# The second mixer's output projection in two column pairs: one more seven-product unit, and other homes for its sums, its recombined input and its spare weight buffer

## The chip, the cores and the metric

The kernel runs on one core of a Trainium2 chip, in one launch. The metric is the device time of that core in microseconds (us). The core's engines run side by side and wait for each other through semaphores: PE (TensorE, the matrix products), DVE (VectorE), ACT (ScalarE), POOL (GpSimd), and SP, which here only issues DMA transfers. On-chip memory is SBUF; products add up in PSUM banks.

## The reference

An encoder of two layers over 256 positions and a model width of 2048, all in float32: layer 0 has grouped-query attention, layer 1 a mixture of dilated window attentions, and each is followed by a gated MLP. The change lies in the last line of the second layer's mixer:

```python
wts = jax.nn.softmax(jnp.stack(log_zs, axis=0), axis=0)
y = jnp.concatenate([wts[g][..., None] * outs[g] for g in range(n_g)], axis=2)
y = y.reshape(b, s, B_WIDTH).astype(h.dtype)
return y @ w_o
```

`y` has 256 rows and 3072 columns (three groups of eight heads of 128), `w_o` is 3072 by 2048. The result is added to the residual `h`, and the MLP of that layer follows, with a root-mean-square norm before it.

## The kernel before

**Split products.** Every float32 factor is split into a rounded high part and a low remainder, and a product is three matrix products: high by high, high by low, low by high. The input's parts lie ready. A weight tile of 128 x 1024 (512 KB) is loaded into a buffer `raw` by SP, then ACT rounds it into `wh` (line 147 or 182) and DVE makes `wl = raw - wh` (line 148 or 183). There are four `wh` and four `wl` buffers (`NHL`), so a split can begin when PE is done with the tile four places before it.

**Plain chunks.** The projection's depth of 3072 is six chunks of 512 (`kg` 0 to 5), its width four column blocks of 512 (`n`). One chunk of one block is a call of `feed`: two loads, two splits, and 24 matmuls (four depth steps, two halves of the 256 rows, three products), so 12 matmuls a weight tile. Chunk `2*g+hf` is made by attention group `g` in half `hf` of the heads, so chunks 0, 2, 4 are there early, and 1, 3, 5 come from the last value stage, which runs beside the start of this projection.

**Seven-product units.** `fast_unit` takes one chunk for two column blocks at once, as a two-by-two matrix product of blocks (rows halves by column blocks) done with seven products in place of eight (Winograd's form of Strassen's scheme): 42 matmuls in place of 48. It loads the same four weight tiles, but makes four sums of them on DVE (line 181: into three `sum` tiles named by `spot`, and one in place), and splits seven tiles in place of four; each split tile serves six matmuls. It needs the chunk's input in a recombined form, `recombined(kg, ...)`: two additions (line 927), four subtractions of half their size (line 934) and one split (lines 323 and 324), kept in `own` tiles. `pair` runs a column pair: it keeps four accumulators (two row halves for each block) and, from the first unit on, four more PSUM banks for products 1, 5, 6 and 7. After the pair's last unit `closing` folds these four into the result (lines 202 to 214: one copy on ACT, four sums on DVE from PSUM, four additions to `h`), beside the accumulators' own additions to `h` (line 464).

**The stage before the change.** Blocks 0 and 1 go through `project2`: chunks 0, 2, 4 for block 0, then for block 1; then all that is left of the value stage is issued and the recombinations of chunks 0 and 2 are started; then chunks 1, 3, 5 for block 0 and for block 1. All of it is plain. Then `pair` runs blocks 2 and 3: chunks 1 and 3 plain for both, chunk 0 as a unit, chunk 4 plain for both, chunk 2 as a unit, chunk 5 plain for both. When a block is added to `h`, ACT takes its sums of squares (line 370) and `late_transpose` turns it into the next stage's input: DVE transposes (line 380), copies of 32 x 256 by POOL (line 399) and ACT (line 401), and a split per 128 columns (lines 334 and 337).

**Weight buffers.** `raw_tile` hands out four `raw` buffers in turn; while `extra[0]` names a pool and tags, every third tile is put into one of those instead. In blocks 0 and 1 there are only the four; in blocks 2 and 3 the tags are `e0` and `e1` (both free once the value stage's `v12` tiles are read), so six buffers, each used again six tiles later. The scheduler sets the order on every engine, SP's queue included, from the order in which the code runs and a head start (`AHEAD`) for the splits. SP's queue is served in its order, and a load waits there until its buffer's last reader is done.

Of the kernel before, what the change touches and what calls it, by code (L numbers as in the profile page):

```python
# [36 lines left out]
def tile_encoder(ctx: ExitStack, tc: tile.TileContext, x, xT, w_a, w_ao, q_gain, k_gain, w_b, w_bo,  # L37
# [25 lines left out]
    def nm(s):  # L63
        uid[0] += 1
        return f"{s}_{uid[0]}"
# [15 lines left out]
    def start(gen):  # L81
        if next(gen, StopIteration) is not StopIteration:
            pending.append(gen)
# [242 lines left out]
    def split(hi, lo, src):  # L326
        if lo is None:
            copy(hi, src)
            return
        nc.scalar.activation(hi, src, AF.Copy)  # L330
        nc.vector.tensor_tensor(lo, src, hi.bitcast(F32), ALU.subtract)  # L331
# [16 lines left out]
    def pair_tile(pool, shape, tag, bufs=1, whole=False):  # L348
        if whole:
            return pool.tile(shape, F32, tag=tag + "h", name=nm(tag), bufs=bufs), None  # L350
        return tuple(pool.tile(shape, F32R, tag=tag + c, name=nm(tag + c), bufs=bufs) for c in "hl")
# [542 lines left out]
    def out_proj(w, slots, kgs, late, g_next, junk, pool, tag, new_quad, cuts=(), units=None):  # L894
        hTn, ss = {}, new_ss()

        def post(n):
            sumsq_cols(ss, n, junk)
            start(late_transpose(hTn, n, g_next, pool, tag, new_quad))

        def done(accs, n):
            add_residual(accs, n)
            post(n)

        if units:
            fast, own, tmp, spot, folds, raws = units
            done(project2(w, 0, 1, slots, kgs, late, lambda a: done(a, 0), None, cuts,
                          [lambda kg=kg: recombined(kg, slots, own, tmp) for kg in fast]), 1)
            extra[0] = raws
            both = {kg: [(kg, 0), (kg, 1)] for kg in sorted(kgs) if kg not in fast}  # L910
            (k0, k1, k2, k3), (f0, f1) = both, fast
            pair(w, (2, 3), slots, both[k0] + both[k1] + [(f0, None)] + both[k2] + [(f1, None)] + both[k3],
                 spot, folds, post)
            extra[0] = None
            drain(1)
            return hTn, ss
        done(project2(w, 0, 1, slots, kgs, late, lambda a: done(a, 0), None, cuts), 1)
        for n in (2, 3):
            done(project(w, n, slots, kgs), n)
        return hTn, ss  # L920
# [330 lines left out]
    def mixer_b(hT, ss_in):  # L1251
        with tc.tile_pool(name="bpool", bufs=1) as bp:
# [34 lines left out]
            def fold_tile():  # L1287
                return bp.tile([P, 2, 512], F32, tag="vh", name=nm("fold"))

            cw, turn = load_taps(1)  # L1290
            allp = slice(None)
            for hf in range(2):
# [77 lines left out]
                def value_stage(hf=hf, probs=probs, e=e, vs=vs):  # L1370
# [40 lines left out]
                    def times_v(g, heads):  # L1411
                        for i in heads:
                            if i % 2 == 0:
                                outs[g] = ps_tile()
                            o = outs[g][:, i % 2 * NT:(i % 2 + 1) * NT]
                            pT = pTs.pop(i) if g == 0 else turned.pop((g, i))
                            for kt in range(2):
                                sel = (allp, kt, slice(i * P, (i + 1) * P))
                                if g == 0:
                                    mm3(o, vs[g], pT, sel, (allp, slice(kt * NT, (kt + 1) * NT)), kt == 0, kt == 1)  # L1420
                                else:
                                    nc.tensor.matmul(o[:, kt * P:(kt + 1) * P], vs[g][0][sel],  # L1422
                                                     pT[:, kt * P:(kt + 1) * P], start=True, stop=True)
                        for i in heads:
                            sl = (2 * g + hf) * 4 + i
                            if i % 2 == 0:
                                slots.update(new_slots((sl, sl + 1)))
                            split(*slots[sl], outs[g][:, i % 2 * NT:(i % 2 + 1) * NT])

                    yield  # L1430
                    for n in range(2):
# [21 lines left out]
                    for g in (1, 2):  # L1453
                        for i in range(0, 4, 2):
                            times_v(g, (i, i + 1))
                            yield
                        if g == 1:
                            yield

                for g in range(3):  # L1460
                    bts = biases(hf, g)
# [27 lines left out]
                    if g == 0:  # L1489
                        start(value_stage())  # L1490

            def own(kg):
                return pair_tile(bp, [P, 4, NT], "qT" if kg else "kT")

            def spot(i):
                t = ("vh", 1) if i == 0 else ("pT", 2)
                return bp.tile([P, 2, 512], F32, tag=t[0], name=nm("sum"), bufs=t[1])

            def folds():
                return [bp.tile([P, 2, 512], F32, tag=t, name=nm("fold")) for t in ("btg", "vh")]  # L1500

            return *out_proj(w_bo, slots, [0, 2, 4, 1, 3, 5], 3, 3, junk, bp, "vl", lambda: quad_tile(bp, "stg", 2),
                             (), ((0, 2), own, tmp, spot, folds, (bp, ["e0", "e1"]))), cw

    hT, ss, cw = mixer_a()
    hT, ss = ffn(0, hT, ss, cw, 2, False, bias_lines)
# [86 lines left out]
```

## Time and profile before

| what | value |
|---|---|
| time, median of 3 runs | 2223.64 us (2222.51 to 2224.64) |
| profiled execution: its time | 2222.29 us |
| profiled execution: its span | 2220.5 us |
| PE busy, share of the span | 2207.1 us, 99% |
| DVE busy | 1823.1 us, 82% |
| ACT busy | 1528.2 us, 69% |
| loads of `w_bo` | 48, of 512 KB |

The span runs from the first to the last instruction; the execution's time holds 1.8 us more around it. PE's busy share counts pipelined matmuls, whose records overlap: the distance from one start to the next is what one more costs. The projection of the change lies between 1374.9 us (its first product) and about 1510 us. A row of the timeline reads: start, duration, engine, line, operation, tiles written and read, count, and in brackets the idle time before it and what ended it.

### The profile page before, as it was taken

What the parts mean: (1) busy time and instruction counts of PE and PEld (TensorE: products, weight loads), DVE (VectorE), ACT (ScalarE), POOL (GpSimd) and SP (SyncE); (2) the same over time, 40 slices, a digit from 0 to 9 for tenths busy, and PEclk for the clock granted to TensorE, in tenths of its full rate; (3) what the DMA queues carried; (4) which work ended last, traced back from release to release, by engine and by line L of the source; (5) the groups of instructions that cost most, each with busy time, mean ns of one, the idle gap of its engine ahead of it and who ended that gap; (6) DMA issues with size and microseconds to landing.
All of it is one profiled execution on the core that took longest, in us unless ns stands there. A gap on an engine that the chain in (4) does not pass through costs nothing.

```text
span 2220.5 us, 28992 instructions
## 1 busy us (share of the span) xinstructions
PE 2207.1 (99%) x9933; PEld 1828.5 (82%) x9933; DVE 1823.1 (82%) x2295; ACT 1528.2 (69%) x2328; POOL 546.1 (25%) x793
## 2 busy tenths in 40 slices
PE   9999999999999999999999999999999999999998
PEld 7888888888888888888888888888888888888887
DVE  6877669899897998868876878587798998879887
ACT  7666677787457787677756775567777855678764
POOL 3343222321003221042354216003222300212211
PEclk9999999999999999999999999999999999999999
DMA  8665665656656566665666555556555565656754
GB/s 305 192 220 184 216 188 190 201 189 196 203 181 222 186 205 200 204 202 195 183 199 199 174 180 189 190 184 214 181 202 194 192 209 190 217 162 218 224 193 143
DMA packets 126181, 439.60 MB, mean 198 GB/s; under 512 B 14408, under 2 KB 18248, under 8 KB 126032
## 3 DMA queue, kind: packets, MB, share of 16 engines
q1 hardware_dynamic: 123056, 429.05, 59.2%
q0 software_dynamic: 2688, 8.39, 1.5%
q8 instruction: 78, 1.28, 0.2%
q14 instruction: 71, 0.58, 0.1%
q10 hardware_dynamic: 288, 0.30, 0.0%
HBM read 432.34 MB, written 5.34 MB: 197 GB/s over the span
## 4 chain that ended last, share of the span: by engine, by line
PE 54%; POOL 1%; issue 1%; DMA 0%; ACT 0%; DVE 0%; POOLq 0%; DVEq 0%; ACTq 0%
PE acc L136 15%; PE acc L135 15%; PE acc L137 15%; PE ps L190 1%; PE ps L189 1%; PE ps L191 1%; PE acc L190 1%; PE acc L189 1%; PE acc L191 1%; DMA raw<-in_w_b_dram 0%; POOL wide L399 0%; PE ps L1422 0%; PE ps L342 0%; POOL wide L384 0%; ACT wh L147 0%
## 5 line engine op out<-in xcount | busy, mean ns | idle before, releaser
L148 DVE TENSOR_TENSOR wl<-raw,wh 128x1024 fp32r<-128x1024 f32 (+1 forms) x700 | 858.9, 1237 | 257.6 <-ACT wh L147 253.1
L147 ACT ACTIVATE wh<-raw 128x1024 fp32r<-128x1024 f32 (+1 forms) x700 | 726.8, 1046 | 342.5 <-PE acc L137 240.6
L136 PE MATMUL acc<-wl,xh 128*128 128x512 f32 x1984 | 773.8, 390 | 1.5 <-DVE wl L148 1.4
L135 PE MATMUL acc<-wh,xh 128*128 128x512 f32 x1984 | 773.7, 390 | 0.5 <-ACT wh L147 0.5
L137 PE MATMUL acc<-wh,xh 128*128 128x512 f32 x1984 | 772.1, 389 | 0.0
L136 PEld LDWEIGHTS acc<-wl,xh 128*128 128x128 f32 x1984 | 372.6, 188 | 81.5 <-DVE wl L148 5.7
L135 PEld LDWEIGHTS acc<-wh,xh 128*128 128x128 f32 x1984 | 372.5, 188 | 77.4 <-ACT wh L147 1.0
L137 PEld LDWEIGHTS acc<-wh,xh 128*128 128x128 f32 x1984 | 372.4, 188 | 76.9
L632 POOL COPY u<-quad 32x256 f32<-32x256 f32 x352 | 237.7, 675 | 702.5 <-DVE quad L380 684.4
L135 PE MATMUL acc<-wh,a 128*128 128x512 f32 x720 | 280.9, 390 | 0.0
L136 PE MATMUL acc<-wl,a 128*128 128x512 f32 x720 | 280.3, 389 | 0.0
L137 PE MATMUL acc<-wh,a 128*128 128x512 f32 x720 | 280.0, 389 | 0.0
L182 ACT ACTIVATE wh<-raw 128x1024 fp32r<-128x1024 f32 x140 | 148.5, 1061 | 122.4 <-PE acc L137 102.6
L183 DVE TENSOR_TENSOR wl<-raw,wh 128x1024 fp32r<-128x1024 f32 x140 | 166.9, 1218 | 6.3 <-ACT wh L182 5.8
L632 ACT ACTIVATE u<-quad 32x256 f32<-32x256 f32 x352 | 147.8, 420 | 23.2 <-DVE quad L380 18.7
L137 PEld LDWEIGHTS acc<-wh,a 128*128 128x128 f32 x720 | 135.1, 188 | 28.3 <-DVE a L331 0.2
L135 PEld LDWEIGHTS acc<-wh,a 128*128 128x128 f32 x720 | 135.2, 188 | 27.7
L136 PEld LDWEIGHTS acc<-wl,a 128*128 128x128 f32 x720 | 135.2, 188 | 27.6 <-DVE wl L148 0.3
L399 POOL COPY wide<-quad 32x256 f32<-32x256 f32 x88 | 54.8, 622 | 234.8 <-DVE quad L380 167.8
L492 ACT ACTIVATE stg<-acc,rstd 128x512 f32<-128x512 f32 x122 | 81.9, 685 | 32.9 <-PE acc L137 21.3
L384 POOL COPY wide<-quad 32x256 f32<-32x256 f32 x133 | 89.8, 675 | 41.4 <-DVE quad L380 32.0
L380 DVE STREAM_TRANSPOSE quad<-stg 128x512 f32<-128x512 f32 x112 | 75.7, 696 | 11.6 <-ACT stg L492 11.4
(318 smaller groups left out, 2444.5 us busy)
## 6 DMA issues: line engine op xcount, KB each, us to landing
raw<-in_w_up_dram SPq DMA_DIRECT2D x352, 512.0 KB, 4.6
raw<-in_w_down_dram SPq DMA_DIRECT2D x176, 512.0 KB, 4.6
raw<-in_w_b_dram SPq DMA_DIRECT2D x144, 512.0 KB, 4.6
raw<-in_w_bo_dram SPq DMA_DIRECT2D x48, 512.0 KB, 4.4
raw<-in_w_a_dram SPq DMA_DIRECT2D x40, 512.0 KB, 4.7
raw<-in_w_ao_dram SPq DMA_DIRECT2D x32, 512.0 KB, 4.5
raw<-in_w_a_dram SPq DMA_DIRECT2D x16, 256.0 KB, 5.8
there<-quad POOLq DMA_DIRECT2D x6, 512.0 KB, 3.7
```

Source lines behind the costliest of these rows:

```text
L135: nc.tensor.matmul(accs[m], xh, wh[:, j, :], start=st, stop=False)
L136: nc.tensor.matmul(accs[m], xh, wl[:, j, :], start=False, stop=False)
L137: nc.tensor.matmul(accs[m], xl, wh[:, j, :], start=False, stop=sp)
L147: nc.scalar.activation(wh[:, c], r[:, c], AF.Copy)
L148: newest[0] = nc.vector.tensor_tensor(wl[:, c], r[:, c], wh[:, c].bitcast(F32), ALU.subtract)
L182: nc.scalar.activation(wh, r, AF.Copy)
L183: newest[0] = nc.vector.tensor_tensor(wl, r, wh.bitcast(F32), ALU.subtract)
L380: nc.vector.transpose(quad[:, :, at, :], src.rearrange("p (x c t) -> p c x t", c=4, t=32))
L384: nc.gpsimd.tensor_copy(o[32 * c:32 * c + 32, :, 32 * q:32 * q + 32], quad[32 * q:32 * q + 32, c])
L399: nc.gpsimd.tensor_copy(dst, src)
L492: evac[0] = nc.scalar.activation(o[:, m, :], accs[m], AF.Copy, scale=rstd[:, m:m + 1])
L632: put(u[32 * c:32 * c + 32, :, :, 32 * q:32 * q + 32], quad[32 * q:32 * q + 32, c].rearrange("p (j m) t -> p j m t", m=2))
```

## The change

Blocks 0 and 1 become a `pair` too, with chunk 2 as a seven-product unit in it; the second pair keeps its two units (chunks 0 and 2). The recombination of chunk 2 (`made(2)`) is put beside the value stage as soon as that has made the last heads of group 0 (chunk 1); that of chunk 0 is started between the two pairs. Chunks are marked in `ready` when they are made, and `pair` issues pending work until the chunk that it wants is marked. The homes change: the recombined inputs move from `kT`/`qT` to `qT` (chunk 0) and `v` (chunk 2); the first weight sum from `vh` to `kTh`; the second fold tile from `vh` to `kTl`; the wide tile of the transposed blocks from `vl` to `e1`. The spare weight buffer is then `e0` alone, named twice, so that it has one place: every third weight tile, from the end of the value stage on, goes into this one place. In `mixer_b`:

```diff
+            ready = {0, 4}
+
+            def made(kg):
+                def own(kg):
+                    return [bp.tile([P, 4, NT], F32R, tag=("v", "qT")[kg == 0] + c, name=nm("own")) for c in "hl"]
+
+                yield from recombined(kg, slots, own, tmp)
+                ready.add(kg)
+
+            def spot(i):
+                t = ("kTh", 1) if i == 0 else ("pT", 2)
+                return bp.tile([P, 2, 512], F32, tag=t[0], name=nm("sum"), bufs=t[1])
+
+            def folds():
+                return [bp.tile([P, 2, 512], F32, tag=t, name=nm("fold")) for t in ("btg", "kTl")]
...
+                        if heads[-1] == 3 and hf == 1:
+                            ready.add(2 * g + hf)
+                            if g == 0:
+                                beside.append(made(2))
...
+                    if hf == 1:
+                        ready.add("u")
+                        extra[0] = bp, ["e0", "e0"]
...
-            def own(kg):
-                return pair_tile(bp, [P, 4, NT], "qT" if kg else "kT")
-
-            def spot(i):
-                t = ("vh", 1) if i == 0 else ("pT", 2)
-                return bp.tile([P, 2, 512], F32, tag=t[0], name=nm("sum"), bufs=t[1])
-
-            def folds():
-                return [bp.tile([P, 2, 512], F32, tag=t, name=nm("fold")) for t in ("btg", "vh")]
-
-            return *out_proj(w_bo, slots, [0, 2, 4, 1, 3, 5], 3, 3, junk, bp, "vl", lambda: quad_tile(bp, "stg", 2),
-                             (), ((0, 2), own, tmp, spot, folds, (bp, ["e0", "e1"]))), cw
+            return *out_proj(w_bo, slots, [0, 2, 4, 1, 3, 5], 3, 3, junk, bp, "e1", lambda: quad_tile(bp, "stg", 2),
+                             (), (made, spot, folds, ready)), cw
```

In `out_proj`:

```diff
         if units:
-            fast, own, tmp, spot, folds, raws = units
-            done(project2(w, 0, 1, slots, kgs, late, lambda a: done(a, 0), None, cuts,
-                          [lambda kg=kg: recombined(kg, slots, own, tmp) for kg in fast]), 1)
-            extra[0] = raws
-            both = {kg: [(kg, 0), (kg, 1)] for kg in sorted(kgs) if kg not in fast}
-            (k0, k1, k2, k3), (f0, f1) = both, fast
-            pair(w, (2, 3), slots, both[k0] + both[k1] + [(f0, None)] + both[k2] + [(f1, None)] + both[k3],
-                 spot, folds, post)
+            made, spot, folds, ready = units
+            both = {kg: [(kg, 0), (kg, 1)] for kg in kgs}
+            pair(w, (0, 1), slots, both[0] + both[4] + both[1] + both[3] + [(2, None)] + both[5], spot, folds, post,
+                 0, ready)
+            ready.discard(0)
+            start(made(0))
+            pair(w, (2, 3), slots, both[1] + both[3] + [(0, None)] + both[4] + [(2, None)] + both[5],
+                 spot, folds, post, 0, ready)
             extra[0] = None
             drain(1)
             return hTn, ss
```

What stands where now, at the places that the prediction speaks of. In these rows a weight tile's name ends in the number of its allocation; `wl` is a split, `sum` and a `raw` written from `raw` are the unit's sums.

First, DVE at the first column pair's fifth chunk. Before, in a plain stretch of block 1:

```order
L148 TENSOR_TENSOR wl_2435_12926<-raw_2429_12902,wh_2434_12925 128x1024
L934 TENSOR_TENSOR tmp_2415_12821<-tmp_2414_12820,tmp_2415_12821 128x256 x2
L148 TENSOR_TENSOR wl_2441_12953<-raw_2438_12948,wh_2440_12952 128x1024
L148 TENSOR_TENSOR wl_2443_12971<-raw_2439_12950,wh_2442_12970 128x1024
L148 TENSOR_TENSOR wl_2447_12993<-raw_2444_12988,wh_2446_12992 128x1024
```

Now, from the third plain tile before the unit to the unit's fourth split:

```order
L148 TENSOR_TENSOR wl_2421_12851<-raw_2417_12832,wh_2420_12850 128x1024
L148 TENSOR_TENSOR wl_2425_12871<-raw_2422_12866,wh_2424_12870 128x1024
L181 TENSOR_TENSOR sum_2436_12914<-raw_2432_12906,raw_2435_12912 128x1024
L148 TENSOR_TENSOR wl_2427_12887<-raw_2423_12868,wh_2426_12886 128x1024
L183 TENSOR_TENSOR wl_2440_12918<-raw_2432_12906,wh_2439_12917 128x1024
L181 TENSOR_TENSOR raw_2435_12912<-raw_2435_12912,raw_2434_12910 128x1024
L183 TENSOR_TENSOR wl_2442_12928<-raw_2433_12908,wh_2441_12927 128x1024
L181 TENSOR_TENSOR sum_2437_12915<-sum_2436_12914,raw_2434_12910 128x1024
L183 TENSOR_TENSOR wl_2444_12938<-raw_2434_12910,wh_2443_12937 128x1024
L181 TENSOR_TENSOR sum_2438_12916<-sum_2437_12915,raw_2433_12908 128x1024
L183 TENSOR_TENSOR wl_2446_12949<-sum_2436_12914,wh_2445_12948 128x1024
```

A stretch with splits and little else now holds the unit's sums between its splits. `raw_2423_12868` and `raw_2434_12910` share the one place `e0`: the second is loaded when the split that reads the first (`wl_2427_12887`) is done.

Second, DVE at the last unit of the second pair (chunk 2). Before, from the last two plain tiles on:

```order
L148 TENSOR_TENSOR wl_2534_13412<-raw_2531_13407,wh_2533_13411 128x1024
L148 TENSOR_TENSOR wl_2536_13428<-raw_2532_13409,wh_2535_13427 128x1024
L181 TENSOR_TENSOR sum_2541_13451<-raw_2537_13443,raw_2540_13449 128x1024
L183 TENSOR_TENSOR wl_2545_13455<-raw_2537_13443,wh_2544_13454 128x1024
L181 TENSOR_TENSOR raw_2540_13449<-raw_2540_13449,raw_2539_13447 128x1024
L183 TENSOR_TENSOR wl_2547_13465<-raw_2538_13445,wh_2546_13464 128x1024
L181 TENSOR_TENSOR sum_2542_13452<-sum_2541_13451,raw_2539_13447 128x1024
```

Now, from the plain stretch's first split on:

```order
L148 TENSOR_TENSOR wl_2539_13392<-raw_2536_13387,wh_2538_13391 128x1024
L148 TENSOR_TENSOR wl_2541_13408<-raw_2537_13389,wh_2540_13407 128x1024
L148 TENSOR_TENSOR wl_2549_13440<-raw_2546_13435,wh_2548_13439 128x1024
L337 SCALAR_TENSOR_TENSOR xh_2542_13423<-wide_2529_13338,gain_76,xh_2542_13423 128x256
L337 SCALAR_TENSOR_TENSOR xh_2543_13426<-wide_2529_13338,gain_76,xh_2543_13426 128x256
L337 SCALAR_TENSOR_TENSOR xh_2544_13429<-wide_2529_13338,gain_76,xh_2544_13429 128x256
L337 SCALAR_TENSOR_TENSOR xh_2545_13432<-wide_2529_13338,gain_76,xh_2545_13432 128x256
L148 TENSOR_TENSOR wl_2551_13456<-raw_2547_13437,wh_2550_13455 128x1024
L181 TENSOR_TENSOR sum_2556_13479<-raw_2552_13471,raw_2555_13477 128x1024
L183 TENSOR_TENSOR wl_2560_13483<-raw_2552_13471,wh_2559_13482 128x1024
L183 TENSOR_TENSOR wl_2562_13493<-raw_2553_13473,wh_2561_13492 128x1024
L181 TENSOR_TENSOR raw_2555_13477<-raw_2555_13477,raw_2554_13475 128x1024
```

The four splits of a transposed block now stand between the units, and `raw_2536_13387`, `raw_2547_13437` and `raw_2554_13475` share `e0`.

Third, SP's queue at the same place, before:

```order
L125 DMA raw_2525_13371<-in_w_bo_dram 128x1024
L125 DMA raw_2526_13373<-in_w_bo_dram 128x1024
L125 DMA raw_2531_13407<-in_w_bo_dram 128x1024
L125 DMA raw_2532_13409<-in_w_bo_dram 128x1024
L170 DMA raw_2537_13443<-in_w_bo_dram 128x1024
```

and now:

```order
L125 DMA raw_2537_13389<-in_w_bo_dram 128x1024
L125 DMA raw_2546_13435<-in_w_bo_dram 128x1024
L125 DMA raw_2536_13387<-in_w_bo_dram 128x1024
L170 DMA raw_2552_13471<-in_w_bo_dram 128x1024
L170 DMA raw_2553_13473<-in_w_bo_dram 128x1024
L125 DMA raw_2547_13437<-in_w_bo_dram 128x1024
L170 DMA raw_2555_13477<-in_w_bo_dram 128x1024
```

The loads stood in the order of use; now the loads into `e0` (13387, 13437) stand two or three places later than their use, behind loads into the four other buffers.

## The prediction

> **What bounds the kernel now.** I read the page's busy shares first, then what PE waited for in the stage, then busy time by stretch, and last the timelines of DVE, ACT and SP's loads around the second pair, where two units of the new kind already run.
>
> ```profile
> span 2220.5 us, 28992 instructions
> PE 2207.1 (99%) x9933; PEld 1828.5 (82%) x9933; DVE 1823.1 (82%) x2295; ACT 1528.2 (69%) x2328; POOL 546.1 (25%) x793
> ```
>
> ```profile
> PE acc L136 <- DVE wl L148: 0.3, 1, 0.3
> ```
>
> ```profile
> core 0: us, PE busy (x) PEld busy (x) DVE busy (x) ACT busy (x) POOL busy (x), PEclk, DMA share, GB/s
> 1410.00:1457.00 47.00, 47.00 (x210) 38.89 (x209) 32.41 (x39) 32.25 (x51) 8.97 (x16) 1.00 0.58 189
> 1457.00:1499.00 42.00, 42.00 (x187) 34.79 (x186) 37.78 (x34) 24.30 (x24) 0.00 (x0) 1.00 0.56 180
> ```
>
> PE bounds: it is idle for 2220.5 - 2207.1 = 13.4 us of the whole span, and between 1340 and 1560 us, around the projection, it waits once, for 0.3 us. So there is next to nothing to win but the products themselves. The two stretches show what a unit costs the others: in plain chunks (1410 to 1457) DVE has 47.0 - 32.4 = 14.6 us free, with two units in 42 us (1457 to 1499) 4.2 us.
>
> ```profile
> 1465.61 0.39 PE L189 MATMUL ps<-wh,a 128*128 128x512 f32 x1
> ...
> 1467.64 0.39 PE L189 MATMUL acc<-wh,a 128*128 128x512 f32 x1
> ```
>
> Between these starts lie nine matmuls: (1467.64 - 1465.61) / 9 = 0.226 us each, though each record is 0.39 us long. A plain weight tile (12 matmuls) keeps PE 2.71 us, a tile of a unit (6) 1.36 us.
>
> ```profile
> 1457.25 1.23 DVE L181 TENSOR_TENSOR sum<-raw,raw 128x1024 f32<-128x1024 f32 x1 [0.88 <-DMA raw<-in_w_bo_dram]
> 1458.39 1.22 DVE L148 TENSOR_TENSOR wl<-raw,wh 128x1024 fp32r<-128x1024 f32 x1
> 1459.53 1.22 DVE L181 TENSOR_TENSOR raw<-raw,raw 128x1024 f32<-128x1024 f32 x1
> 1460.66 1.22 DVE L181 TENSOR_TENSOR sum<-sum,raw 128x1024 f32<-128x1024 f32 x1
> 1461.80 1.22 DVE L183 TENSOR_TENSOR wl<-raw,wh 128x1024 fp32r<-128x1024 f32 x1
> ...
> 1479.94 1.23 DVE L181 TENSOR_TENSOR sum<-raw,raw 128x1024 f32<-128x1024 f32 x1 [2.29 <-DMA raw<-in_w_bo_dram]
> ```
>
> ```profile
> 1457.64 1.06 ACT L182 ACTIVATE wh<-raw 128x1024 fp32r<-128x1024 f32 x1 [1.58 <-PE acc L137]
> ```
>
> ```profile
> DMA to landing us min/median/max: 3.6/4.4/5.5
> ```
>
> A DVE sum or split takes 1.22 us, but the next starts after 1.14 (1458.39, 1459.53, 1460.66). ACT's rounding takes 1.06 and waits for PE to leave the buffer four tiles back. A load of 512 KB lands 3.6 to 5.5 us after its issue, 4.4 in the median of the 48. Both units already make DVE wait for a load, 0.88 and 2.29 us, with six buffers; PE does not feel it.
>
> **The change part by part.** *Products.* One chunk of blocks 0 and 1 takes 42 matmuls in place of 48: 6 x 0.226 = 1.36 us less on PE, the engine that sets the end. (The mean busy time of 0.39 would make it 2.3; the spacing is what counts.) The second pair keeps its units, so this is all.
>
> *DVE and ACT.* The new unit has 7 splits for 4, and 4 sums: 7 more operations, 7 x 1.14 = 8.0 us on DVE; on ACT three more roundings, 3 x 1.06 = 3.2 us. Closing the pair adds the eight operations of lines 204 to 214.
>
> ```profile
> 1502.48 0.68 DVE L210 TENSOR_TENSOR h<-h,fold 128x512 f32<-128x512 f32 x1
> 1503.08 0.68 DVE L211 TENSOR_TENSOR h<-h,fold 128x512 f32<-128x512 f32 x1
> 1503.68 1.30 DVE L380 STREAM_TRANSPOSE quad<-h 128x512 f32<-128x512 f32 x2
> ```
>
> At 0.60 from start to start they are 4.8 us. Together 12.8 us, against the 14.6 that DVE had free in the plain stretch: covered on average, with little over. On ACT the 3.2 us and one copy lie in 47.0 - 32.3 = 14.7 us of idle time. If that cover were gone, every 1.14 us of DVE would be 1.14 us on PE.
>
> *Order.* Chunk 1 is wanted after eight tiles in place of twelve, 8 x 2.71 = 21.7 us after the first product at 1374.91, so at 1396.6; chunk 3 at 1407, chunk 5 later still.
>
> ```profile
> 1376.05 0.38 DVE L331 TENSOR_TENSOR a<-ps,a 128x256 fp32r<-128x256 f32 x1
> ...
> 1394.61 0.42 DVE L331 TENSOR_TENSOR a<-ps,a 128x256 fp32r<-128x256 f32 x1 [0.45 <-ACT a L330]
> ```
>
> The first row ends chunk 1, the second chunk 5, the last of all. Nothing is late: I cost this at nothing. The recombinations are the same two; that of chunk 2 moves into DVE's idle time before 1400, that of chunk 0 stands between the pairs. Loads are the same 48, and the homes taken over (`kTh`, `kTl`, `vl`'s successor `e1`) belong to the value stage that is over by then: nothing.
>
> *The spare buffer* is the term that can cost. With `e0` alone, every third tile has one place, so its load waits for the split three tiles earlier, then come landing, ACT's 1.06 and DVE's split: 4.4 + 1.06 + 1.22 = 6.7 us a round, against 3 x 2.71 = 8.1 us of plain PE work, but only 4.1 us in a unit. Before, each place had six tiles' time. And DVE works in order: a sum that waits for such a load holds up all splits behind it. I follow the three units by hand in the order of rows shown above, with 4.4 us of landing.
>
> *Unit of the first pair.* Let PE leave the seventh plain tile before the unit at time 0. ACT and DVE finish the third-last tile (`wl_2421`) at 1.06 + 1.22 = 2.3; that frees the place for the unit's `raw_2435`, which lands at 6.7; its sum ends at 7.8, the last plain split (`wl_2427`) at 9.0; only now is `e0` free for `raw_2434`: 13.4. The sum into `raw_2435` waits for it; with the operations behind it up to the fourth split (`wl_2446`) that is 6 x 1.14: 20.2. PE has six plain tiles and three of the unit until then, 16.3 + 4.1, and needs the low part one matmul later: 20.6. Margin 0.4 us; and the landing stands in it twice.
>
> *First unit of the second pair.* The start is the same, to 9.0 us; its four sums then stand early and the load into `e0` is in time. Its fourth split comes after five more operations, two, four and one small ones between, at about 19.2: margin 1.4. But POOL's sixteen copies of two transposed blocks fall here.
>
> ```profile
> 1447.86 1.40 DVE L148 TENSOR_TENSOR wl<-raw,wh 128x1024 fp32r<-128x1024 f32 x1 [0.67 <-ACT wh L147]
> ```
>
> Beside such copies a split took 1.40, not 1.22. For nine operations that is 1.6 us: a loss of about 0.2 us, from 0 to 0.5. The Trainium skill ("SBUF — State Buffer", Who interferes with whom) says more: a VectorE operation with two SBUF inputs and a GpSimd operation that reads SBUF share a port pair, and the second to issue "fully blocks" until the first is done. The row above shows 0.18 us of it; what full blocking would give is a rival below.
>
> *Second unit of the second pair.* Let DVE finish the unit before at time 0, with PE just waiting for it. The first plain split ends at 1.14 and frees `e0`; `raw_2547` lands at 5.5, is rounded at 6.6 and split at 7.8 (the other two splits and the four of line 337 fit in between). `raw_2554` lands at 12.2; the sum that waits for it and four more operations end the fourth split at 12.2 + 5.7 = 17.9. PE needs it after 1.36 + 4 x 2.71 + 3 x 1.36 + 0.2 = 16.5. So PE waits 1.4 us, less what lead the unit before left it (some 0.4). Again two landings are in it.
>
> *Sum.* At 4.4 us: 0 + 0.2 + 1.0 = 1.2 us of new waits. With loads as fast as 3.6: none. With 5.5: 1.8 + 1 + 3.6 = 6.4. In a unit loads come in fours, and run into each other:
>
> ```profile
> DMA to landing us min/median/max: 3.7/4.9/5.5
> ```
>
> These are the loads issued between 1460 and 1480, in the second pair. Some of the loads into `e0` will have company, some not; I take 4.6: 0.1 + 0.3 + 1.6 = 2.0 us. So -1.36 + 2.0 = +0.6 us: the span becomes 2221.1. The profiled execution took 2222.29, which is 1.35 under the median of the three; from the median, 2223.64 + 0.6 = 2224.2 us. The bounds: 2223.64 - 1.4 = 2222.3 and 2223.64 - 1.4 + 6.4 = 2228.6.
>
> *Between the pairs* PE's first matmul into block 2 waits for block 0's additions to `h` (line 464), which stand on DVE behind five splits and the fold's four sums; the fifth split reads `e0` again. Counted from the unit's last split: two splits to 2.3, load and rounding to 7.8, split 8.9, addition 9.5; PE gets there after the unit's last tile and four plain ones, 1.4 + 10.8 = 12.2. Margin 2.7 us: nothing.
>
> **The rivals.** *The products are simply saved.* If the loads into `e0` land in under 4.1 us, or DVE gains lead elsewhere, no unit waits: 2222.3 us. For it: PE felt nothing of the waits of 0.88 and 2.29 us. Against: those had six places. The Trainium skill ("DMA: Bandwidth & Descriptors", Anatomy of one DMA) fits 2.0 us + bytes/436e3, an estimate of 3.2 us for 512 KB on GpSimd's path; the fastest here took 3.6, so by the trace it is not that quick.
>
> *The single place decides (slower).* If the landings of the loads that share `e0` average 5.2 us or more, the first and the last unit each lose two times the excess: at 5.3, 1.4 + 0.9 + 3.2 = 5.5; and in plain chunks the round of 5.3 + 2.3 = 7.6 us leaves only 0.5 of 8.1 to catch up, so that a lag of the first pair is carried into the second, 1 us more: -1.4 + 6.5 = +5.1, 2228.7 us. For it: the maximum of 5.5, and 4.9 as the median of twenty microseconds. Against: a place that is served late makes fewer loads run side by side.
>
> *POOL's copies block DVE.* Were every one of the nine operations held for half a copy (the eight at 1447.35 took 4.35 us, 0.54 each, so 0.3), that is 2.4 us more in the second pair's first unit and, its lead gone, 0.4 in the next: 2224.2 + 2.4 = 2226.6.
>
> ```profile
> 1447.35 4.35 POOL L399 COPY wide<-quad 32x256 f32<-32x256 f32 x8 [10.02 <-DVE quad L380]
> ```
>
> *It gains more than the products,* because the reordering also takes away waits: these are 0.3 us in the whole stage, so a gain of over 0.2% is not to be had this way.
>
> **How the numbers follow.** The forecast has 0.48, the plain saving 0.24, the single place 0.18, the blocking copies 0.08, a larger gain 0.02. About 0.2% (4.4 us) is what a measurement of this kernel can tell from no change. Faster by more: 0.02. Slower by more, over 2228.1: the single place, and a little of the others: 0.19. Within: 0.79. The range goes from the plain saving with half a microsecond of the runs' own spread, 2221.8, to 2228.8, a little past the single place's price, and leaves out about 0.1 at each end.
>
> **What would show it.** Right: PE with six matmuls fewer; in the first pair's unit and in the second pair's last one, PE waiting for DVE's `wl` of line 183 for some tenths to 1.5 us, and ahead of it DVE idle for a load of `w_bo` at line 181, 3 us and more, the load issued only when the split three tiles before was done. Wrong: PE waits at line 135 or 1438 (readiness, the order), at lines 202 to 214 or 464 (the accumulators come free late), or DVE never idle for loads while PE waits. The forecast itself is wrong if PE's new waits in the stage are under 0.7 or over 5.8 us.

## The result, and the profile after

| kernel | time, median | range | runs |
|---|---|---|---|
| before | 2223.64 us | 2221.76 to 2225.1 | 11 |
| changed | 2230.2 us | 2225.22 to 2232.12 | 11 |

The ratio is 1.0028, 95% interval 1.0020 to 1.0035: the changed kernel is slower by 0.28%, 6.6 us between the medians. Predicted were 2224.2 us and a range to 2228.8. The profiled execution took 2229.77 us.

The page of the changed kernel, span and busy line:

```profile
span 2228.0 us, 29016 instructions
PE 2209.2 (99%) x9927; PEld 1827.7 (82%) x9927; DVE 1834.0 (82%) x2310; ACT 1530.5 (69%) x2332; POOL 548.1 (25%) x793
```

The six matmuls are gone (9933 to 9927). What PE waited for between 1340 and 1560 us (engine, tile and line, what ended the wait; us in total, times, longest), where it had waited once for 0.3 us:

```profile
PE ps L190 <- DVE wl L183: 2.8, 4, 0.9
PE acc L190 <- DVE wl L183: 1.3, 3, 0.6
PE acc L136 <- DVE wl L148: 1.0, 1, 1.0
```

Line 190 is a unit's matmul with the low part: in a unit PE waits seven times for DVE's split. Line 136 is here a product of the MLP behind the projection, with a late split, some 9 us after the MLP's first product (1513.30 us); that place is called "the joint" below. Busy time by stretch tells where; the columns are the stretch and its length, then busy time of PE, weight loads, DVE, ACT and POOL, and the granted clock. First before, then after:

```profile
1440.00:1460.00 20.00, 20.00 (x90) 16.57 (x89) 15.48 (x21) 14.57 (x25) 4.06 (x8) 1.00 0.58 185
1460.00:1480.00 20.00, 20.00 (x90) 16.57 (x89) 16.29 (x15) 11.69 (x11) 0.00 (x0) 1.00 0.65 206
```

```profile
1400.00:1440.00 40.00, 40.00 (x178) 33.06 (x177) 28.16 (x27) 18.17 (x19) 0.00 (x0) 1.00 0.57 184
1440.00:1460.00 20.00, 20.00 (x90) 16.57 (x89) 18.68 (x25) 13.77 (x23) 4.65 (x5) 1.00 0.64 192
1460.00:1480.00 20.00, 16.93 (x69) 11.95 (x68) 16.41 (x17) 13.60 (x22) 11.11 (x11) 1.00 0.45 150
1480.00:1500.00 20.00, 18.95 (x82) 14.85 (x81) 17.82 (x19) 13.71 (x19) 1.07 (x2) 1.00 0.58 186
1500.00:1525.00 25.00, 24.03 (x107) 19.56 (x105) 23.82 (x34) 19.07 (x35) 9.71 (x15) 1.00 0.48 155
```

The clock is the same. PE loses most between 1460 and 1480, in the first unit of the second pair, and less in the second unit and at the joint. DVE is no busier there than before (16.41 and 16.29), so it is not short of time: it waits too. POOL, which had nothing to do there, now works for 11.11 us. The timelines of POOL, ACT and DVE in the changed kernel show what they wait for:

```profile
1455.18 9.02 POOL L399 COPY wide<-quad 32x256 f32<-32x256 f32 x8 [72.86 <-PE acc L137]
1472.72 8.39 POOL L399 COPY wide<-quad 32x256 f32<-32x256 f32 x8 [8.52 <-DVE quad L380]
```

```profile
1458.87 2.13 ACT L401 ACTIVATE wide<-quad 32x256 f32<-32x256 f32 x5
1464.23 0.51 ACT L334 ACTIVATE xh<-wide,gain 128x256 fp32r<-128x256 f32 x1 [3.24 <-POOL wide L399]
1464.65 1.04 ACT L182 ACTIVATE wh<-raw 128x1024 fp32r<-128x1024 f32 x1
...
1472.65 0.84 ACT L401 ACTIVATE wide<-quad 32x256 f32<-32x256 f32 x2 [2.92 <-DVE quad L380]
1473.52 1.06 ACT L182 ACTIVATE wh<-raw 128x1024 fp32r<-128x1024 f32 x1
```

```profile
1462.52 1.42 DVE L181 TENSOR_TENSOR sum<-sum,raw 128x1024 f32<-128x1024 f32 x1
1465.72 1.23 DVE L183 TENSOR_TENSOR wl<-raw,wh 128x1024 fp32r<-128x1024 f32 x1 [1.79 <-ACT wh L182]
...
1474.61 1.26 DVE L183 TENSOR_TENSOR wl<-raw,wh 128x1024 fp32r<-128x1024 f32 x1 [0.94 <-ACT wh L182]
```

Read from the bottom: DVE's first split of the unit waits 1.79 us for ACT's rounding (line 182). That rounding stands in ACT's queue behind the scaled split of block 0's transposition (line 334), which waits 3.24 us for POOL's eight copies; and these took 9.02 us. Later ACT is stopped again, 2.92 us, by block 1's first copy, which waits for DVE's transposition (line 380), and that stands on DVE between the unit's splits. Before, POOL's eight copies had taken 5.20 us for block 0 and 4.35 for block 1 (1447.35 to 1451.70), and all were over when the unit began at 1465.61. Block 0's, before:

```profile
1432.13 5.20 POOL L399 COPY wide<-quad 32x256 f32<-32x256 f32 x8 [49.66 <-DVE quad L380]
```

**A finer yardstick.** Single runs of one kernel differ by up to 7 us, more than what is to be told apart. The table under the experiments therefore also has the length of the stage in each trace: from the start of one matmul ahead of the projection (1372.15 us before) to the start of the same matmul in the MLP behind it (1600.18 us), 228.03 us before. Changed: 1373.66 to 1607.81, 234.15 us, so +6.12. The products alone would make it 1.36 shorter; 6.12 + 1.36 = 7.48 us is lost to waits. The rest of the 7.5 us between the two profiled spans lay already ahead of the stage (1373.66 against 1372.15). By a gap I mean what lies between two matmul starts beyond the 0.227 us of their spacing: in the changed kernel 3.9 us in the first unit of the second pair, 1.4 in its second unit, 1.1 at the joint (0.45 before); what is left of the 7.5 are delays of under a quarter of a microsecond each.

### The profile page after: what moved, and what is told of

It is laid out like the page before. It is cut to its first block, busy times and chain, and to the rows that moved or that the text cites. A ratio compares the mean times of both kernels' runs of the same rounds, so it can differ in the third digit from the quotient of the medians.

```text
span 2228.0 us, 29016 instructions
## 1 busy us (share of the span) xinstructions
PE 2209.2 (99%) x9927; PEld 1827.7 (82%) x9927; DVE 1834.0 (82%) x2310; ACT 1530.5 (69%) x2332; POOL 548.1 (25%) x793
## 4 chain that ended last, share of the span: by engine, by line
PE 51%; DVE 2%; POOL 1%; issue 1%; DMA 1%; ACT 1%; POOLq 0%; DVEq 0%; ACTq 0%
PE acc L136 14%; PE acc L135 14%; PE acc L137 14%; PE ps L190 1%; PE ps L191 1%; PE ps L189 1%; PE acc L190 1%; PE acc L191 1%; PE acc L189 1%; POOL wide L399 1%; DMA raw<-in_w_b_dram 0%; DVE wl L148 0%; PE ps L1438 0%; PE ps L342 0%; DVE wl L183 0%
## 5 line engine op out<-in xcount | busy, mean ns | idle before, releaser
L135 PE MATMUL acc<-wh,a 128*128 128x512 f32 x704 | 274.7, 390 | 0.0
L136 PE MATMUL acc<-wl,a 128*128 128x512 f32 x704 | 274.2, 390 | 0.0
L137 PE MATMUL acc<-wh,a 128*128 128x512 f32 x704 | 273.8, 389 | 0.0
L183 DVE TENSOR_TENSOR wl<-raw,wh 128x1024 fp32r<-128x1024 f32 x144 | 171.9, 1218 | 8.5 <-ACT wh L182 8.1
L137 PEld LDWEIGHTS acc<-wh,a 128*128 128x128 f32 x704 | 132.1, 188 | 27.5 <-DVE a L331 0.2
L135 PEld LDWEIGHTS acc<-wh,a 128*128 128x128 f32 x704 | 132.2, 188 | 27.1
```

What stands on the lines that cost most here:

```text
L135: nc.tensor.matmul(accs[m], xh, wh[:, j, :], start=st, stop=False)
L136: nc.tensor.matmul(accs[m], xh, wl[:, j, :], start=False, stop=False)
L137: nc.tensor.matmul(accs[m], xl, wh[:, j, :], start=False, stop=sp)
L183: newest[0] = nc.vector.tensor_tensor(wl, r, wh.bitcast(F32), ALU.subtract)
```

## The experiments

Theory A is the one place of the spare weight buffer, on which the prediction rested. Theory B is the reading above: ACT's in-order queue, blocked by the transposition of blocks 0 and 1. Later came B2 (it matters how late the blocks are finished), C (the new unit's own work) and D (DVE has no time left). "Lost" is the stage's difference plus 1.36 us where the unit saves its products. Each median is of 5 to 11 runs; each ratio is to the runs of the kernel before in the same series, whose medians were 2223.64 to 2224.36 us; each stage is that of one trace.

| kernel | median, us | ratio to before (95%) | stage | lost |
|---|---|---|---|---|
| before, one spare place | 2223.84 | 1.0002 (0.9993 to 1.0011) | -0.01 | 0.0 |
| changed | 2230.2 | 1.0028 (1.0020 to 1.0035) | +6.12 | 7.5 |
| changed, two spare places | 2228.08 | 1.0020 (1.0011 to 1.0028) | +3.86 | 5.2 |
| changed, transposition behind the unit | 2229.69 | 1.0032 (1.0020 to 1.0043) | +4.89 | 6.3 |
| the same, two spare places | 2229.93 | 1.0027 (1.0016 to 1.0037) | +5.85 | 7.2 |
| changed, no copies on POOL | 2232.03 | 1.0034 (1.0022 to 1.0046) | +6.77 | 8.1 |
| changed, first pair plain | 2227.69 | 1.0017 (1.0009 to 1.0026) | +2.98 | 3.0 |
| changed, early recombination | 2232.36 | 1.0034 (1.0021 to 1.0046) | +7.04 | 8.4 |
| changed, blocks two chunks apart | 2226.79 | 1.0013 (1.0004 to 1.0022) | +1.68 | 3.0 |
| changed, blocks four chunks apart | 2223.88 | 0.9999 (0.9990 to 1.0007) | -0.71 | 0.7 |
| the same kernel again | 2223.68 | 0.9997 (0.9988 to 1.0006) | -0.70 | 0.7 |
| four chunks apart, two spare places | 2223.67 | 1.0000 (0.9991 to 1.0009) | -0.86 | 0.5 |
| four chunks apart, early recombination | 2223.6 | 0.9995 (0.9986 to 1.0004) | -0.82 | 0.5 |

**One spare place in the kernel before.**

```diff
-                             (), ((0, 2), own, tmp, spot, folds, (bp, ["e0", "e1"]))), cw
+                             (), ((0, 2), own, tmp, spot, folds, (bp, ["e0", "e0"]))), cw
```

> The kernel before, with its spare weight buffer of the second column pair cut from two places to one; nothing else is changed. Theory A (the single place alone makes the units late): new waits of PE in the second pair's two units of 1.4 to 4 us against none before, and the time up by as much, to 2225 - 2227.6 us. Theory B (what hurts is the transposition of blocks 0 and 1, which the change puts in front of and into the second pair's first unit: ACT's in-order queue stands behind slowed POOL copies): in this kernel that transposition lies elsewhere, so PE waits at most 0.5 us and the time stays within 1 us of 2223.6.

PE's waits between 1340 and 1560 us are those of before:

```profile
PE acc L136 <- DVE wl L148: 0.3, 1, 0.3
```

The stage has the same length within 0.01 us. Theory A alone falls: with the order of before, the one place costs nothing.

**Two spare places in the changed kernel.** The second is made of the input tiles 14 and 15, joined into one of 4 KB.

```diff
-                        extra[0] = bp, ["e0", "e0"]
+                        extra[0] = bp, ["e0", "x14"]
```

> The changed kernel with a second place for the spare weight buffer (space of two tiles of the old input that are free by then); nothing else is changed. Theory A: the 3.9 us of PE gaps in the first unit of the second pair and the 1.4 us in its last unit both fall under 0.5, the time falls by some 5 us to 2224 - 2225. Theory B: the first unit keeps at least 3 of its 3.9 us, since ACT's rounding still stands behind the scaled split that waits for POOL; only the last unit's 1.4 us go; 2227.5 - 2229.

2.3 us of the 7.5 go, 1.7 of them in the first unit. The same two stops stand in ACT's timeline (3.28 us at line 334, 2.92 us at line 401). The result lies between the theories: B's cause stays, and the second place takes away part of its effect. Theory B's 2227.5 to 2229 holds, though the first unit loses less than the 3 us it asked for: PE's gaps there fall from 3.9 to 2.2 us; and the second unit, whose 1.4 us both theories had let go, keeps 1.1.

**Transposition behind the unit.** ACT's copies are held in program order, and block 0's transposition starts eight turns later; block 1's is queued behind it.

```diff
-            start(late_transpose(hTn, n, g_next, pool, tag, new_quad))
+            start(itertools.chain([None] * (8 if units and n == 0 else 0), late_transpose(hTn, n, g_next, pool, tag, new_quad)))
...
-                nc.scalar.activation(dst, src, AF.Copy)
+                pin(nc.scalar.activation(dst, src, AF.Copy))
```

> The changed kernel with ACT's share of the transposition of blocks 0 and 1 (its copies, and with them the scaled splits of lines 334 and 337) put behind the first unit of the second pair; the spare buffer keeps its one place. POOL's copies may still run beside the unit. Theory B: the first unit's 3.9 us of PE gaps fall under 1.0, the last unit's 1.4 us stay or grow by up to 1 because its surroundings get the work; 2226 - 2228. Theory A: the first unit keeps at least 3 us, no gain over 1 us.

> Both edits together: two places, and ACT's share of the transposition behind the first unit. If A and B together are the whole account, no unit waits more than 0.5 us, the sum of PE gaps in the stage falls from 6.4 to under 1.7 (the joint to the MLP keeps its 1.1), and the time is 2222.3 - 2224, at or under the kernel before. If a third cause is at work (DVE has too little time left in the second pair), at least 2 us of gaps stay in the units.

PE's waits with one place:

```profile
PE acc L136 <- DVE wl L148: 5.0, 3, 2.5
PE ps L190 <- DVE wl L183: 0.4, 1, 0.4
```

The first unit waits no more, as B expected, although POOL's first eight copies are as slow and as late as in the changed kernel (9.95 us from 1453.24, to 0.9 us ahead of the unit's first product), and the second unit's gaps fall to 0.6. But the work comes back at the joint: block 1's transposition now meets those of blocks 2 and 3, and PE waits 5.0 us for the MLP's first splits. The time of 2229.69 is above B's range. With two places the units also wait only 0.4 us, and the joint costs 4.6: the forecast of 2222.3 to 2224 was wrong, since both expectations had left out that the work must end ahead of the MLP.

**All copies of blocks 0 and 1 on ACT.**

```diff
-                quad_place(o, quad, range(i, i + 8), EVEN)
+                quad_place(o, quad, range(i, i + 8), () if g == 3 and n < 2 else EVEN)
```

> The changed kernel with all sixteen copies of each of blocks 0 and 1 on ACT (8 more each, 0.42 us a piece, 3.4 us a block) and none on POOL. If POOL's slowed copies (9.0 us for eight) are what holds the scaled split and with it ACT's first rounding of the unit: the gap of 0.97 us at the unit's first split and part of those behind it go, the unit's gaps fall from 3.9 to 1 - 2.5. If ACT itself is the limit there, they stay or grow by up to 3 us (2230 - 2233).

PE's gaps in the first unit fall from 3.9 to 2.4 us, and the one at its first split is gone: POOL was what held that rounding. The second unit's grow from 1.4 to 2.6. ACT carries 8 x 0.42 us more a block; that this makes the rest and the second unit late is my reading of it. The first unit's gaps are in the range for POOL as the cause, the time is in that for ACT as the limit: in sum nothing is won.

**First pair plain.** Chunk 2 is plain for both blocks, 48 matmuls, and there is no fold behind the pair.

```diff
-            pair(w, (0, 1), slots, both[0] + both[4] + both[1] + both[3] + [(2, None)] + both[5], spot, folds, post,
+            pair(w, (0, 1), slots, both[0] + both[4] + both[1] + both[3] + both[2] + both[5], spot, folds, post,
...
+            post(0)
+            post(1)
```

> The changed kernel with the first pair's unit taken out again: chunk 2 is plain for both blocks (48 matmuls), there is no fold after the pair; both blocks still end 5.4 us apart at its end, the spare buffer keeps its one place. Theory B2: the gaps of the second pair's first unit stay at 2 to 4 us; with the 1.36 us of products back the time is 2227 - 2231. Theory C (the new unit's own work on DVE, above all its fold, makes the second pair late): these gaps fall under 1, 2223.5 - 2226.

POOL's copies of blocks 0 and 1 now lie here:

```profile
1443.32 4.33 POOL L399 COPY wide<-quad 32x256 f32<-32x256 f32 x8 [59.51 <-PE acc L137]
1453.69 5.20 POOL L399 COPY wide<-quad 32x256 f32<-32x256 f32 x8 [6.04 <-DVE xh L337]
```

The time is within B2's range, but the first unit's gaps are 1.2 us, between the two expectations. Without a unit there is no fold, and without the fold the transposition comes 12 us earlier (1443.32 against 1455.18). What is lost is 3.0 us, not 7.5. So the new unit's work does count (C), most likely by delaying the transposition.

**Early recombination.** The recombination of chunk 0 is started ahead of the first pair.

```diff
+            start(made(0))
             pair(w, (0, 1), slots, both[0] + both[4] + both[1] + both[3] + [(2, None)] + both[5], spot, folds, post,
                  0, ready)
-            ready.discard(0)
-            start(made(0))
```

> The changed kernel with the recombination of chunk 0 (two additions, four subtractions and one split on DVE, 4.2 us in all, between 1430 and 1457 us) started ahead of the first pair and not behind it; the blocks still end one chunk apart, one spare place. Theory D (between 1430 and 1462 us DVE has no time left: fold, additions to h, recombination and transposition are all due there, and what is late is handed on to the unit): with 4.2 us less the second pair's first unit loses 1.5 us or less in place of 3.9, the time is 2225 - 2228. If only the transpositions count, its gaps stay over 3 us, 2228.5 or more.

Theory D falls: DVE has 4.2 us less to do ahead of the unit, and the loss grows to 8.4 us. The case shows the mechanism almost alone. PE's waits, POOL's copies, ACT and DVE, and the stretch from 1474 to 1476 us (its last three columns: granted clock, DMA share, GB/s):

```profile
PE acc L189 <- ACT wh L182: 4.0, 1, 4.0
PE acc L136 <- DVE wl L148: 1.0, 1, 1.0
PE acc L190 <- DVE wl L183: 0.5, 1, 0.5
```

```profile
1451.80 5.42 POOL L399 COPY wide<-quad 32x256 f32<-32x256 f32 x8 [67.88 <-ACT wh L147]
1461.88 8.38 POOL L399 COPY wide<-quad 32x256 f32<-32x256 f32 x8 [4.66 <-DVE xh L337]
```

```profile
1465.45 0.84 ACT L401 ACTIVATE wide<-quad 32x256 f32<-32x256 f32 x2
1470.29 1.31 ACT L334 ACTIVATE xh<-wide,gain 128x256 fp32r<-128x256 f32 x3 [4.00 <-POOL wide L399]
1471.50 1.04 ACT L182 ACTIVATE wh<-raw 128x1024 fp32r<-128x1024 f32 x1
```

```profile
1470.83 0.48 DVE L337 SCALAR_TENSOR_TENSOR xh<-wide,gain,xh 128x256 fp32r<-128x256 f32 x1 [2.58 <-ACT xh L334]
1472.57 1.23 DVE L183 TENSOR_TENSOR wl<-raw,wh 128x1024 fp32r<-128x1024 f32 x1 [1.26 <-ACT wh L182]
```

```profile
1474.00:1476.00 2.00, 2.00 (x5) 1.61 (x6) 2.00 (x4) 1.78 (x2) 0.00 (x0) 0.50 0.43 125
```

PE waits 4.0 us for one rounding, and ACT, which should do it, waits 4.00 us at line 334 for POOL, while DVE is idle as well. Not all of the 8.4 us is waiting: behind this stop PE's granted clock is 0.50 to 0.52 until 1478 us, and twelve matmul starts from 1473.85 on take 5.19 us and not 2.72. These 2.5 us explain why this run loses more than the changed kernel, although its copies end earlier; without them the first unit's gaps are some 5 us. The second row of POOL shows one thing more: the two blocks share the one `wide` tile, so block 1's copies wait for block 0's scaled splits (line 337). Two blocks finished together are transposed one after the other, and the second runs into the unit.

**The blocks further apart.** The one spare place and all numbers of instructions stay; only the order in the first pair changes, so that block 0 is finished four chunks ahead of block 1 and not one. With that the unit comes after five plain chunks and not after eight (its first product at 1406.41 us and not 1423.60), and its fold earlier too:

```diff
-            pair(w, (0, 1), slots, both[0] + both[4] + both[1] + both[3] + [(2, None)] + both[5], spot, folds, post,
+            pair(w, (0, 1), slots, [(0, 0), (4, 0), (0, 1), (1, 0), (3, 0), (2, None), (5, 0), (4, 1), (1, 1), (3, 1), (5, 1)], spot, folds, post,
```

> The changed kernel with the plain chunks of the first pair in another order, so that block 0 is finished four chunks (21.6 us) ahead of block 1 and not one (5.4 us); the unit, the one spare place and all else stay. Theory B2 (the loss comes from both blocks being finished at the pair's very end, so that both transpositions run into the second pair's first unit): that unit's 3.9 us of PE gaps fall under 1.0; the last unit may keep its 1.4; time 2223.5 - 2226. Theory A (the one place): the gaps of the units stay at 3 us or more in sum, 2227 - 2230, and the first pair's unit, which now has block 0's chunk behind it, may wait too.

> The same order, and a second place for the spare buffer. B2 and A together: gaps in the units under 0.5 us in sum, joint to the MLP as before (0.5) or as now (1.1): 2222.3 - 2223.6, at or under the kernel before. If a third cause is at work: 2 us or more of gaps stay.

PE's waits, POOL's copies and a row of DVE in the second unit, with one spare place:

```profile
PE acc L136 <- DVE wl L148: 0.8, 1, 0.8
```

```profile
1432.26 5.54 POOL L399 COPY wide<-quad 32x256 f32<-32x256 f32 x8 [50.80 <-issue]
1448.47 6.21 POOL L399 COPY wide<-quad 32x256 f32<-32x256 f32 x8 [10.68 <-DVE quad L380]
```

```profile
1480.14 1.23 DVE L181 TENSOR_TENSOR sum<-raw,raw 128x1024 f32<-128x1024 f32 x1 [0.62 <-DMA raw<-in_w_bo_dram]
```

No unit waits, in any of the four traces with four chunks; with two places the median is 0.07 us above what was expected. Both transpositions are over before the first product of the second pair's first unit, and DVE's 0.62 us for a load does not reach PE. The second spare place changes the stage by 0.15 us: here too the one place costs next to nothing. Of the 1.36 us saved, 0.7 to 0.9 us are left; the joint takes the rest. With half the distance:

```diff
+            pair(w, (0, 1), slots, both[0] + both[4] + [(1, 0), (3, 0), (3, 1), (2, None), (5, 0), (1, 1), (5, 1)], spot, folds, post,
```

> The changed kernel with block 0 finished two chunks (10.8 us) ahead of block 1: half way between the changed kernel (one chunk, 6.4 us of gaps in the stage) and the run with four chunks (1.0). By theory B2 the loss falls with the distance: block 0's transposition gets out of the unit, block 1's scaled split still stands ahead of the unit's first rounding on ACT. Gaps of 1 to 3.5 us in the stage, time 2224.5 - 2227. If only the chunk right behind the unit mattered, they would be as with one chunk, over 5 us.

> The same kernel as the run with four chunks of distance, once more, for a narrower comparison with the kernel before: the products saved (1.36 us) less the longer wait at the joint to the MLP (0.5) should leave 0.8 us, 0.04%, so a ratio of 0.9996 with an interval that still touches 1.

> Early recombination and four chunks of distance together: no unit waits (0 to 0.3 us of gaps), the joint to the MLP keeps its 0.9 to 1.1; as with the distance alone, 2222.5 - 2224, ratio to the kernel before 0.9993 to 1.

All three came out as expected. Half way the waits are

```profile
PE ps L190 <- DVE wl L183: 1.3, 2, 1.0
PE acc L136 <- DVE wl L148: 1.0, 1, 1.0
```

and POOL's last copy of block 1 ends at 1456.49 + 6.17 = 1462.66 us, 4.7 us ahead of the unit's first product (1467.40). The same distance makes a row beside the loss: 13.9 us ahead before (0 lost), 10.2 with four chunks (0.7, all of it behind the units), 8.1 with the plain pair (3.0), 4.7 with two chunks (3.0), and 4.5 behind that product with early recombination (8.4, of which 2.5 are the low clock), 13.3 behind with two spare places (5.2), 15.3 behind in the changed kernel (7.5). With a margin of 10 us no unit waits, with less the loss grows, to 5 us and more once the copies run into the unit. How early the transposition ends goes with the loss; the distance between the blocks is one way to it, but the plain pair shows that the unit's fold is another, and no run moved the unit earlier with the blocks left one chunk apart, so the shares of the two are not shown. No median with four chunks is above that of the kernel before in the same series (2223.93 to 2224.36). The gain of 0.7 to 0.9 us, seen in four traces, is 0.03% to 0.04%: no interval of the times excludes 1.

## Why the prediction was wrong, step by step

- *Products:* 1.36 us saved. Right: six matmuls fewer, and with no waits in the units the stage is 0.7 to 0.9 us shorter beside a joint that costs some 0.5 more.
- *DVE and ACT, covered on average.* The sum holds, its place does not. DVE has 11.8 us idle between 1400 and 1440 (28.16 of 40.00 busy), but the fold, the additions and the transposition can only be done when the unit is, and from 1440 to 1460 it is busy for 18.68 of 20. An idle time that lies ahead of the work does not cover it.
- *Order and homes, nothing.* Right for readiness: no wait at lines 135 or 1438 in the stage. What I did not follow is that one chunk, in place of three, now lies between the end of block 0 and that of block 1; so two transpositions fall due together.
- *Unit of the first pair,* 0.1: it lost nothing. DVE was idle for loads as foreseen, 1.97 and 2.74 us at line 181, and PE's lead covered it:

```profile
1414.48 1.23 DVE L181 TENSOR_TENSOR sum<-raw,raw 128x1024 f32<-128x1024 f32 x1 [1.97 <-DMA raw<-in_w_bo_dram]
...
1420.71 1.23 DVE L181 TENSOR_TENSOR raw<-raw,raw 128x1024 f32<-128x1024 f32 x1 [2.74 <-DMA raw<-in_w_bo_dram]
```

- *First unit of the second pair: "a loss of about 0.2 us, from 0 to 0.5".* This is the step that failed. I saw that POOL's sixteen copies fall there and charged them to DVE, 0.18 us an operation. DVE's operations did grow to 1.42 us and no more. The price was elsewhere: POOL's eight copies took 9.02 us, where the 4.35 of the row that I used had been the quicker of the two sets, the scaled split of line 334 waits for them, and the unit's roundings stand behind it in ACT's queue. PE's gaps there are 3.9 us beyond its spacing. I had written that an operation of DVE that waits holds up all splits behind it; the same holds for ACT's queue, and I did not follow it.
- *Second unit,* 1.6: measured 1.4, near by luck as far as is known. The link that I had foreseen is in the trace: the load into `e0` is issued at 1486.63, as soon as the split that frees it is done, and DVE's sum waits 0.45 us for it and ACT's rounding 4.03. But it does not set the price by itself. With early recombination DVE waits the same way (0.52 us) and PE does not; with two places the wait is gone and 1.1 us of gaps stay; with the same one place and the blocks four chunks apart the unit loses nothing. What makes it late in the changed kernel is not shown; block 1's transposition, whose copies end at 1481.11 between the two units, is the nearest candidate.
- *Between the pairs,* nothing: right for PE's accumulators, to which I limited it. The same operations on the way to the transposition were the late ones.
- *The joint* was not in the sum: its gap grew from 0.45 to 1.1 us.

That the forecast of +0.6 us had the right sign is luck: it came from the spare place, which alone costs nothing. The rival of the single place had the side right too (2228.7, slower), but the place alone is refuted as the cause. The rival of POOL's copies named the right place and the right pair of engines, and had the wrong one of them blocked; its sum also leaves out the 0.4 us that it names for the next unit, with which it is 2227.0. Of the signs, PE did wait for `wl` of line 183 in the second pair's units, but not in the first pair's. The limit of 5.8 us for new waits would be kept by the list of waits (5.1 less 0.3) and is passed by the distances between starts (7.5), which also count the slow matmul behind each wait.

Open is why a second spare place takes 2.3 us off the changed order, next to nothing off the kernel before and the order with four chunks, and makes the run with the transposition behind the unit 1.0 us longer (there a lower clock at the joint, below, accounts for more than the difference). That a late split frees its place late, and so passes its lag on to the next load, fits, but was not tried by itself.

## What to carry to other kernels

A piece of work that becomes due only when a block is finished is priced by where it lands, and by every in-order queue that it enters: one instruction that waits for a slow engine holds up all urgent ones behind it. When two blocks are finished together, look for single-place tiles between them and at what engine order the scheduler gives; changing the order of independent chunks so that they end apart can cost nothing and take the whole loss away. Moving late work still later only helps if no joint waits for it.

## What the runs showed of the hardware

**POOL beside DVE.** POOL's eight copies of 32 x 256 took 4.33 to 9.95 us, by what DVE did beside them. A single copy took 0.39 us alone; beside a DVE operation with two inputs in SBUF (lines 148, 181, 183, 324) most took 1.2 to 1.5. Two copies of the changed kernel with DVE's split beside the first, then one of the run with early recombination:

```profile
1456.69 1.42 DVE L148 TENSOR_TENSOR wl<-raw,wh 128x1024 fp32r<-128x1024 f32 x1
1457.07 1.29 POOL L399 COPY wide<-quad 32x256 f32<-32x256 f32 x1
1458.40 0.39 POOL L399 COPY wide<-quad 32x256 f32<-32x256 f32 x1
```

```profile
1461.88 3.53 POOL L399 COPY wide<-quad 32x256 f32<-32x256 f32 x1 [4.66 <-DVE xh L337]
```

The first ends a quarter of a microsecond behind the split, the second begins while DVE is idle; the third lasts through three DVE operations without a pause between them (1461.67 to 1465.15). DVE's operations took 1.42 in place of 1.22 us when a copy ended some 0.3 us after they began, and 1.22 to 1.23 in the same stretch of the run without POOL's copies. Beside additions with one input in PSUM (line 464), in the run with the plain pair, the copies took 0.39. The Trainium skill ("SBUF — State Buffer", Who interferes with whom) says that a VectorE operation with two inputs in SBUF and a GpSimd operation that reads SBUF lock each other out, and that the order of issue decides who is blocked. The trace agrees with the lock, with POOL as the one that pays most; the order alone does not explain the copy of 3.53 us, since two of the three operations beside it began after it. I had not expected that the loser would be the engine with little work, and that it would cost through a third one.

**PE's clock behind a stop.** With early recombination PE stood for 4.1 us, and then ran at a granted clock of 0.50 to 0.52 until 1478 us, with starts 0.427 us apart and not 0.227. In the run with the transposition behind the unit and two spare places a stop of 2.6 us at the joint was followed by 0.50 between 1526 and 1528 us, some 1.6 us lost; with one place a stop of the same 2.6 us was followed by 1.00. What decides this is not shown here; that a stop can cost more than its length is.
